# Down projection of a SwiGLU block as seven block products over all tokens

## The chip, the cores and the metric

One core of a Trainium2 chip. The metric is the device time of one execution in microseconds (us); of three runs of the kernel before, the median is 2898.46 us (2891.17 to 2900.06).

## The reference, cut to what matters

One decoder layer over 2048 prompt tokens and 8 sample tokens, all in float32. The mixer (HGRN2 and differential attention) comes first and is not touched. What follows is the feed-forward part:

```python
def swiglu(h, wg, wu, wd):
    return jnp.einsum('btf,fd->btd', jax.nn.silu(jnp.einsum('btd,df->btf', h, wg))
                      * jnp.einsum('btd,df->btf', h, wu), wd)
# hp = hp + swiglu(rmsnorm(hp, norm_ffn[l]), w_gate[l], w_up[l], w_down[l])
# y_prompt = rmsnorm(hp, norm_final)
# D_MODEL = 1024, D_FF = 2816; prompt 2048 tokens, sample 8 tokens
```

## The kernel before

A float32 product is made of three matmuls on rounded halves: each operand is split into a rounded part (a cast on ScalarE) and a rest (a subtraction on VectorE), and high x high, high x low and low x high are added in PSUM. This split stands behind every matrix product of the kernel, so each weight or token tile costs a cast and a subtraction before TensorE can use it.

**Gate/up** (`gate_up`, line 1171). The 2056 token columns (8 of the sample, then 2048) are cut into three groups of 688, 684 and 684 (`FG`). Per group `b_operands` loads the normed tokens into one staging tile (`xraw`) and makes the seven right operands of Strassen's scheme (Winograd's form: seven products of half-size blocks in place of eight), as 28 tiles `B`. Then for each of eleven pairs of feature tiles (256 features) and for both weights `a_operands` loads a 1024 x 256 block of weights (`raw_gate`, `raw_up`, one buffer each), forms four sums on VectorE and cuts seven left operands (`A`, ten buffers); `strassen` runs seven products of 4 x 3 matmuls with 342 or 344 columns, and VectorE puts the four result blocks together. The weights' sums are thus formed anew in each of the three groups. The features, silu(gate) x up, go to DRAM (`hd`) in two halves per pair.

**Down** (`down`, line 1201). Plain tiles: four groups of 512 tokens, two halves of 512 output columns each, and in each half 22 feature tiles x 4 token tiles x 3 matmuls of 512 columns. A weight tile (128 x 512) is loaded into `wraw` (three buffers), split into `w` (eight buffers) and used for the four token tiles; the 22 feature tiles of a token group are loaded into `hraw` and split into `ha` or `hb`. The eight sample tokens join the second token group as a fifth tile. `result` adds the product to the residual (`ya`), and after the second half norms, scales and stores the rows.

**What sets the order.** Instructions are written in program order; a planner then orders them per engine, giving an instruction its place as soon as its inputs and its buffer are free in its own time table, earlier ones first. Each engine, and SP's queue of DMA issues, then works strictly in that order: an instruction that waits holds up what is behind it. Loads are issued by SP, stores of gate/up by POOL (GpSimd). The buffers of a stage lie in the memory of the stage before; a tile there waits for the release of the tiles that it overlaps: `rb` (right side) holds `xraw`, `xtmp` and the operands `B`, and `rd` takes its place in down; `fa` (left) holds `A`, the raw weights and the feature tiles, and `fd` takes its place.

Of the kernel before, what the change touches and what calls it, by code (L numbers as in the profile page):

```python
# [9 lines left out]
F32 = mybir.dt.float32  # L10
# [9 lines left out]
P = 128  # L20
D = 1024
# [21 lines left out]
def layer_kernel(ctx, tc, x_prompt, x_sample, cache_k, cache_v, state_hgrn, page_table, w_in, w_out,  # L43
# [112 lines left out]
    hd = [[T(dp, [P, 2, b - a], F32, f"hd{a}_{c}") for c in range(NF // 2)] for a, b in FG]  # L156
# [66 lines left out]
    with ExitStack() as mx:  # L223
# [849 lines left out]
        def pieces(a, b):  # L1073

            out = []
            if a < NS:
                out.append((xtd_s, 0, NS, 0))
            for t in range(NT):
                lo, hi = max(a, NS + t * P), min(b, NS + (t + 1) * P)
                if lo < hi:  # L1080
                    out.append((xtd[t], lo - NS - t * P, hi - NS - t * P, lo - a))
            return out

# [8 lines left out]
        def b_operands(g):  # L1092
# [4 lines left out]
            for src, c0, c1, to in pieces(a, b):  # L1097
                sp.dma_start(raw[:, :, to:to + c1 - c0], src[:, :, c0:c1])
# [23 lines left out]
        def a_operands(fa, w, c, raw):  # L1122

            sp.dma_start(raw, w[:, c * 2 * P:(c + 1) * 2 * P].rearrange("(k p) f -> p k f", p=P))
            A11, A21, A12, A22 = (raw[:, k:k + 4, m * P:m * P + P] for k in (0, 4) for m in range(2))
# [7 lines left out]
            def sums(x, y, op):  # L1133
                s_ = T(fa, [P, 4, P], F32, "S", 4)
                dve.tensor_tensor(s_, x, y, op=op)
                return s_

            ops = {1: cut(A11)}
            S1 = sums(A21, A22, ALU.add)
            S2 = sums(S1, A11, ALU.subtract)  # L1140
            ops[6] = cut(S2)
            ops[7] = cut(sums(A11, A21, ALU.subtract))
            ops[5] = cut(S1)
            ops[4] = cut(A22)
            ops[3] = cut(sums(A12, S2, ALU.subtract))
            ops[2] = cut(A12)
            return ops
# [23 lines left out]
        def gate_up(fa):  # L1171
            fill = last_tokens()
            for g, (lo, hi) in enumerate(FG):
# [5 lines left out]
                for c in range(NF // 2):  # L1179
                    sg = [[T(fa, [P, TH], F32, "sg", 5)[:, 0:n] for j in range(2)] for i in range(2)]  # L1180
                    hh = [T(fa, [P, 2 * TH], F32, "hh", 3)[:, 0:2 * n].rearrange("p (j t) -> p j t", j=2) for i in range(2)]
# [5 lines left out]
                    def put_up(i, j, p, u, op):  # L1187
                        dve.tensor_tensor(hh[i][:, j], u, p, op=op)
                        dve.tensor_tensor(hh[i][:, j], hh[i][:, j], sg[i][j], op=ALU.mult)

                    us = [[T(fa, [P, TH], F32, tag, 2)[:, 0:n] for tag in ("s1", "s5", "u2", "u3")] for i in range(2)]
                    raws = [T(fa, [P, KT, 2 * P], F32, tag, 1) for tag in ("raw_up", "raw_gate")]
                    for w, put in ((w_gate, put_gate), (w_up, put_up)):
                        u_ = us.pop()
                        strassen(a_operands(fa, w, c, raws.pop()), B, n, put, u_)
                        pools["first"] = u_[1]
                        next(fill, None)
                    for i in range(2):
                        pool.dma_start(hd[g][c][:, i], hh[i].rearrange("p j t -> p (j t)"))

        def down(fd, rd):

            LATE = 15
            late = [T(rd, [P, 2, 512], F32R, "hb", LATE) for _ in range(LATE)]

# [5 lines left out]
            def weight(f, hs):  # L1211
                raw = T(rd, [P, 512], F32, "wraw", 3)
                sp.dma_start(raw, w_down[f * P:(f + 1) * P, hs])
                return halves(T(rd, [P, 2, 512], F32R, "w", 8), raw)

            def feature(f, c0):
                raw = T(rd, [P, 512], F32, "hraw", 3)
# [127 lines left out]
```

## Time and profile before

| what | value |
|---|---|
| profiled execution | 2899.44 us, span 2897.7 us |
| median of three runs | 2898.46 us |
| TensorE busy | 2790.8 us, 96% of the span |
| VectorE, ScalarE, GpSimd busy | 67%, 48%, 11% |
| bytes moved by DMA | 480.81 MB, 166 GB/s |
| mean granted TensorE clock | 0.982 of full speed |

Busy times overlap between engines. A matmul's listed duration includes its passage through the array, and the next starts before it ends; so the spacing of starts, not the duration, is the cost of one in a stream. A group's line ends with the idle time of the engine just before it and with what ended that idle time.

### The profile page before, as it was taken

What the parts mean: (1) busy time and instruction counts of PE and PEld (TensorE: products, weight loads), DVE (VectorE), ACT (ScalarE), POOL (GpSimd) and SP (SyncE); (2) the same over time, 40 slices, a digit from 0 to 9 for tenths busy, and PEclk for the clock granted to TensorE, in tenths of its full rate; (3) what the DMA queues carried; (4) which work ended last, traced back from release to release, by engine and by line L of the source; (5) the groups of instructions that cost most, each with busy time, mean ns of one, the idle gap of its engine ahead of it and who ended that gap; (6) DMA issues with size and microseconds to landing.
All of it is one profiled execution on the core that took longest, in us unless ns stands there. A gap on an engine that the chain in (4) does not pass through costs nothing.

```text
span 2897.7 us, 44200 instructions
## 1 busy us (share of the span) xinstructions
PE 2790.8 (96%) x16149; PEld 2524.7 (87%) x16149; DVE 1942.6 (67%) x4152; ACT 1393.3 (48%) x3256; POOL 322.3 (11%) x444
## 2 busy tenths in 40 slices
PE   8999999999999999998989999999999999999998
PEld 7887899888888788887779999999999997878886
DVE  6473577676766676862489889988988865525342
ACT  6422277665665656742564445444544434424232
POOL 2373400000000000011210000000000000000000
PEclk9999999999999999999999999999999999999999
DMA  6885896744644533334965333323233337726342
GB/s 226 310 280 174 248 296 197 235 150 148 209 135 143 184 134 134 103 124 151 326 207 170 117 102 123 126 102 110 100 102 107 103 119 239 221 90 228 129 160 77
DMA packets 311487, 480.81 MB, mean 166 GB/s; under 512 B 30659, under 2 KB 226293, under 8 KB 301542
## 3 DMA queue, kind: packets, MB, share of 16 engines
q1 hardware_dynamic: 281862, 364.13, 39.5%
q0 software_dynamic: 29408, 113.85, 10.8%
q8 instruction: 128, 2.10, 0.3%
q14 instruction: 89, 0.73, 0.1%
HBM read 359.81 MB, written 118.09 MB: 165 GB/s over the span
## 4 chain that ended last, share of the span: by engine, by line
PE 70%; issue 15%; DMA 8%; ACT 3%; DVE 2%; POOL 1%; SPq 1%; POOLq 0%; ACTq 0%; DVEq 0%
PE b L1155 10%; PE b L1156 10%; PE b L1157 10%; PE mm L315 7%; PE mm L316 7%; PE mm L317 7%; PE av L453 3%; PE sc L406 2%; PE th L536 2%; PE sc L408 2%; PE tpa L449 2%; PE b L1287 1%; PE b L1289 1%; PE b L1288 1%; DMA xn<-xnd 1%
## 5 line engine op out<-in xcount | busy, mean ns | idle before, releaser
L1155 PE MATMUL b<-B,A 128*128 128x342 f32 (+1 forms) x1848 | 593.5, 322 | 9.4 <-ACT B L1088 7.0
L1157 PE MATMUL b<-B,A 128*128 128x342 f32 (+1 forms) x1848 | 591.2, 320 | 0.7 <-DVE A L1130 0.7
L1156 PE MATMUL b<-B,A 128*128 128x342 f32 (+1 forms) x1848 | 591.0, 320 | 0.0
L315 PE MATMUL mm<-xn,w 128*128 128x512 f32 (+1 forms) x1120 | 405.1, 362 | 6.3 <-ACT hraw L486 3.1
L317 PE MATMUL mm<-xn,w 128*128 128x512 f32 (+1 forms) x1120 | 396.6, 354 | 0.0
L316 PE MATMUL mm<-xn,w 128*128 128x512 f32 (+1 forms) x1120 | 396.2, 354 | 0.0
L1155 PEld LDWEIGHTS b<-B,A 128*128 128x128 f32 x1848 | 350.3, 190 | 12.0 <-ACT B L1088 8.6
L1156 PEld LDWEIGHTS b<-B,A 128*128 128x128 f32 x1848 | 350.9, 190 | 0.0
L1157 PEld LDWEIGHTS b<-B,A 128*128 128x128 f32 x1848 | 349.3, 189 | 1.0 <-DVE A L1130 1.0
L1208 DVE TENSOR_TENSOR w<-wraw,w 128x512 fp32r<-128x512 f32 x176 | 121.2, 690 | 219.4 <-ACT w L1207 219.0
L412 DVE TENSOR_REDUCE nms<-sc 128x1 f32<-128x512 f32 (+3 forms) x320 | 188.3, 605 | 117.4 <-PE sc L408 59.3
L1129 ACT CAST A<-S 128x512 fp32r<-128x512 f32 x264 | 163.2, 621 | 213.0 <-PE b L1157 198.4
L315 PEld LDWEIGHTS mm<-xn,w 128*128 128x128 f32 x1120 | 215.4, 192 | 34.3 <-ACT hraw L486 4.4
L317 PEld LDWEIGHTS mm<-xn,w 128*128 128x128 f32 x1120 | 214.7, 192 | 27.1
L316 PEld LDWEIGHTS mm<-xn,w 128*128 128x128 f32 x1120 | 215.3, 192 | 24.9
L413 ACT ACTIVATE e<-sc,nms 128x512 f32<-128x512 f32 (+3 forms) x320 | 201.6, 635 | 67.4 <-DVE nms L412 65.2
L1207 ACT CAST w<-wraw 128x512 fp32r<-128x512 f32 x176 | 109.2, 621 | 250.5 <-PE b L1289 199.0
L1130 DVE TENSOR_TENSOR A<-S,A 128x512 fp32r<-128x512 f32 x264 | 181.3, 689 | 30.1 <-ACT A L1129 26.5
L1287 PE MATMUL b<-w,hb 128*128 128x512 f32 x480 | 186.2, 390 | 1.8 <-ACT hb L1207 1.8
L1288 PE MATMUL b<-w,hb 128*128 128x512 f32 x480 | 185.8, 389 | 0.0
L1289 PE MATMUL b<-w,hb 128*128 128x512 f32 x480 | 185.4, 390 | 0.0
L453 PE MATMUL av<-vb,pt 128*128 128x128 f32 x1088 | 155.6, 282 | 11.4 <-ACT pt L451 11.2
(379 smaller groups left out, 5558.8 us busy)
## 6 DMA issues: line engine op xcount, KB each, us to landing
w<-wd SPq DMA_DIRECT2D x48, 1024.0 KB, 5.0
wraw<-in_w_down_dram SPq DMA_DIRECT2D x176, 256.0 KB, 2.9
raw_gate<-in_w_gate_dram SPq DMA_DIRECT2D x33, 1024.0 KB
raw_up<-in_w_up_dram SPq DMA_DIRECT2D x33, 1024.0 KB, 5.3
wraw<-in_w_in_dram SPq DMA_DIRECT2D x40, 512.0 KB, 7.0
kb<-kd SPq DMA_DIRECT2D x40, 512.0 KB, 6.2
wd<-w SPq DMA_DIRECT2D x16, 1024.0 KB, 5.5
qst<-qd SPq DMA_DIRECT2D x128, 128.0 KB, 6.5
```

Source lines behind the costliest of these rows:

```text
L315: pe.matmul(bk[:, 0:n], wv[:, 0, kt], xk[:, 0, c0:c1], start=kt == 0, stop=False)
L316: pe.matmul(bk[:, 0:n], wv[:, 0, kt], xk[:, 1, c0:c1], start=False, stop=False)
L317: pe.matmul(bk[:, 0:n], wv[:, 1, kt], xk[:, 0, c0:c1], start=False, stop=kt == KT - 1)
L412: dve.tensor_reduce(nm, sc[:, 0:n], axis=AX.X, op=ALU.max, negate=True)
L413: act.activation(e[m][:, 0:n], sc[:, 0:n], AF.Exp, bias=nm, accum_out=c["z"][:, b, m:m + 1])
L453: pe.matmul(po[:, 0:P], pt[:, j * P:(j + 1) * P], it["v"][b][:, j], start=b == 0 and j == 0, stop=b == nb - 1 and j == n // P - 1)
L1155: pe.matmul(bk[:, 0:n], a[:, 0, k], b[:, 0, 0:n], start=k == 0, stop=False)
L1156: pe.matmul(bk[:, 0:n], a[:, 0, k], b[:, 1, 0:n], start=False, stop=False)
L1157: pe.matmul(bk[:, 0:n], a[:, 1, k], b[:, 0, 0:n], start=False, stop=k == 3)
L1287: pe.matmul(bk[t], h[f][:, 0, ts], w[f][:, 0], start=st, stop=False)
L1288: pe.matmul(bk[t], h[f][:, 0, ts], w[f][:, 1], start=False, stop=False)
L1289: pe.matmul(bk[t], h[f][:, 1, ts], w[f][:, 0], start=False, stop=en)
```

## The change

The features' own block sums are now made in gate/up, and down runs Strassen's scheme over blocks of 1024 tokens x 1408 features x 512 outputs.

- Gate/up: the weights' sums are formed in place in a seven-slot tile in the first group only (`sums7`), stored to DRAM (`wsd`), and loaded from there in the other two groups. `A` has eight buffers instead of ten, and the separate tiles for sums are gone. The features of a pair go into a seven-slot tile `hh`, where `sums7` adds three sums and a difference (four more VectorE operations per pair), and all seven slots are stored (`hd`). The token groups are mapped so that the two halves of a group hold tokens 1024 apart; the sample's features are copied out (`hsd`).
- Down: for each of seven products in the order 1, 6, 7, 5, 4, 3, 2, eight row blocks of 128 tokens x 11 feature pairs x 3 matmuls of 512 columns. The eleven weights of a product are each summed from one to four raw tiles (`SUM`). The features of a row block are one load of 128 x 11 x 128 values in runs of at most 512 bytes. Results stay in sixteen SBUF tiles `Y2` of 128 x 1024; each product is added where it belongs; the residual is added in product 5, rows 1024 to 2047 are finished in product 4 and rows 0 to 1023 in product 2. The sample runs beside the products 1, 5, 3 and 2 with the same weights.

```diff
-    hd = [[T(dp, [P, 2, b - a], F32, f"hd{a}_{c}") for c in range(NF // 2)] for a, b in FG]
+    hd = [T(dp, [P, 7, NF // 2, (b - a) // 2], F32, f"hd{a}") for a, b in FG]
+    hsd = T(dp, [P, NF, NS], F32, "hsd")
+    wsd = [[T(dp, [P, 7, 512], F32, f"wsd{m}_{c}") for c in range(NF // 2)] for m in range(2)]
...
+        def sums7(x):
+            tt = dve.tensor_tensor
+            tt(x[:, 3], x[:, 5], x[:, 1], op=ALU.add)
+            tt(x[:, 4], x[:, 3], x[:, 0], op=ALU.subtract)
+            tt(x[:, 5], x[:, 0], x[:, 5], op=ALU.subtract)
+            tt(x[:, 6], x[:, 2], x[:, 4], op=ALU.subtract)
+        SLOT = {1: 0, 6: 4, 7: 5, 5: 3, 4: 1, 3: 6, 2: 2}
...
-        def a_operands(fa, w, c, raw):
-            sp.dma_start(raw, w[:, c * 2 * P:(c + 1) * 2 * P].rearrange("(k p) f -> p k f", p=P))
+        def a_operands(fa, m, c, raw, g):
+            if g:
+                sp.dma_start(raw, wsd[m][c])
+            else:
+                w = (w_gate, w_up)[m]
+                for slot, k, col in ((0, 0, 0), (5, 0, 1), (1, 1, 1), (2, 1, 0)):
+                    at = (2 * c + col) * P
+                    sp.dma_start(raw[:, slot].rearrange("p (k f) -> p k f", k=4),
+                                 w[k * 512:(k + 1) * 512, at:at + P].rearrange("(k p) f -> p k f", p=P))
             def cut(x):
-                o = T(fa, [P, 2, 4, P], F32R, "A", 10)
+                o = T(fa, [P, 2, 4, P], F32R, "A", 8)
...
+            ops = {1: cut(raw[:, 0])}
+            if g == 0:
+                sums7(raw)
+                pool.dma_start(wsd[m][c], raw)
+            for p in (6, 7, 5, 4, 3, 2):
+                ops[p] = cut(raw[:, SLOT[p]])
...
+                    raws = [T(fa, [P, 7, 512], F32, tag, 1) for tag in ("raw_up", "raw_gate")]
...
+                            hh.append(T(fa, [P, 7, TH], F32, "hh", 2))
...
-                        pool.dma_start(hd[g][c][:, i], hh[i].rearrange("p j t -> p (j t)"))
+                    x = hh[0][:, :, 0:n]
...
+                    sums7(x)
+                    pool.dma_start(hd[g][:, :, c], x)
...
         def down(fd, rd):
+            NC = NF // 2
+            order = (1, 6, 7, 5, 4, 3, 2)
+            SUM = {1: ((0, 0, 1),), 6: ((1, 1, 1), (0, 1, -1), (0, 0, 1)), 7: ((1, 1, 1), (0, 1, -1)),
+                   5: ((0, 1, 1), (0, 0, -1)), 4: ((1, 1, 1), (0, 1, -1), (0, 0, 1), (1, 0, -1)), 3: ((1, 1, 1),), 2: ((1, 0, 1),)}
...
+            def weight(p, c):
+                got = None
+                for k, n, sign in SUM[p]:
+                    raw = T(rd, [P, 512], F32, "wraw", 4)
+                    sp.dma_start(raw, w_down[(2 * c + k) * P:(2 * c + k + 1) * P, n * 512:n * 512 + 512])
+                    if got is not None:
+                        dve.tensor_tensor(got, got, raw, op=ALU.add if sign > 0 else ALU.subtract)
+                    else:
+                        got = raw
+                return halves(T(rd, [P, 2, 512], F32R, "w", 16), got)
...
+            def feature(p, i):
+                raw = T(rd, [P, NC, P], F32, "hraw", 2)
+                for g, c0, c1, _, r in rows(0, i):
+                    sp.dma_start(raw[:, :, r:r + c1 - c0], hd[g][:, SLOT[p], :, c0:c1])
+                return halves(T(rd, [P, 2, NC, P], F32R, "h", 2), raw)
...
+            def residual(h, i):
+                res = T(fd, [P, D], F32, "res", 2)
...
+                y = Y2[h][i]
+                dve.tensor_tensor(y, y, res, op=ALU.add)
...
+            for p in order:
+                W = []
+                for i in range(8):
+                    A = feature(p, i)
+                    bk = bank()
+                    for c in range(NC):
+                        if i == 0:
+                            W.append(weight(p, c))
+                        pe.matmul(bk, A[:, 0, c], W[c][:, 0], start=c == 0, stop=False)
+                        pe.matmul(bk, A[:, 0, c], W[c][:, 1], start=False, stop=False)
+                        pe.matmul(bk, A[:, 1, c], W[c][:, 0], start=False, stop=c == NC - 1)
...
+                    if p == 1:
+                        act.copy(a[0], bk)
+                    elif p == 6:
+                        tt(a[1], a[0], bk, op=ALU.add)
+                    elif p == 7:
+                        tt(b[0], a[1], bk, op=ALU.add)
+                    elif p == 5:
+                        tt(b[1], b[0], bk, op=ALU.add)
+                        tt(a[1], a[1], bk, op=ALU.add)
+                        residual(1, i)
+                        residual(0, i)
...
+                    if p in (4, 2):
+                        h = 1 if p == 4 else 0
...
+                        finish(P, Y2[h][i])
+                        for g, c0, c1, t0, r in rows(h, i):
+                            sp.dma_start(yp[t0:t0 + c1 - c0], Y2[h][i][r:r + c1 - c0])
```

## Rows read from the trace of the kernel before

**Rows 1.** The page, busy time, share of the span and instructions per engine.
```profile
PE 2790.8 (96%) x16149; PEld 2524.7 (87%) x16149; DVE 1942.6 (67%) x4152; ACT 1393.3 (48%) x3256; POOL 322.3 (11%) x444
```

**Rows 2.** Stretches: length, busy per engine (instructions), granted clock, DMA share, GB/s.
```profile
1488.50:2376.60 888.10, 880.09 (x5560) 877.28 (x5560) 773.91 (x1388) 411.14 (x791) 38.92 (x70) 0.99 0.34 113
2376.60:2885.00 508.40, 502.39 (x2201) 409.04 (x2200) 216.62 (x318) 177.40 (x314) 17.07 (x18) 1.00 0.52 170
...
2110.00:2200.00 90.00, 90.00 (x576) 90.00 (x575) 79.36 (x143) 38.90 (x74) 4.32 (x8) 1.00 0.34 114
```

**Rows 3.** Groups by line and shape, TensorE in the down projection.
```profile
L1287 PE MATMUL b<-w,hb 128*128 128x512 f32 x480 | 186.2, 390 | 1.8 <-ACT hb L1207 1.8
...
L1287 PE MATMUL b<-w,ha 128*128 128x512 f32 x224 | 86.1, 391 | 4.2 <-ACT ha L1207 4.2
```

**Rows 4.** Timeline of TensorE around the stages' border: start, duration, engine, line, tiles.
```profile
2373.11 0.32 PE L1157 MATMUL b<-B,A 128*128 128x342 f32 x1
...
2376.40 0.32 PE L1157 MATMUL b<-B,A 128*128 128x342 f32 x1
2380.04 1.29 PE L1287 MATMUL b<-w,ha 128*128 128x512 f32 x4 [3.32 <-ACT ha L1207]
...
2384.48 1.08 PE L1287 MATMUL b<-w,ha 128*128 128x512 f32 x4
...
2388.58 0.39 PE L1287 MATMUL b<-w,ha 128*128 128x512 f32 x1
...
2391.53 0.39 PE L1288 MATMUL b<-w,ha 128*128 128x512 f32 x1
```

**Rows 5.** Timeline of VectorE at the start of gate/up, operations back to back.
```profile
1495.43 0.69 DVE L1130 TENSOR_TENSOR A<-raw_gate,A 128x512 fp32r<-128x512 f32 x1
1496.03 0.69 DVE L1130 TENSOR_TENSOR A<-S,A 128x512 fp32r<-128x512 f32 x1
...
1505.25 0.52 DVE L1184 TENSOR_TENSOR sg<-u,s 128x344 f32<-128x344 f32 x1
1505.68 0.52 DVE L1184 TENSOR_TENSOR sg<-u,b 128x344 f32<-128x344 f32 x1
```

**Rows 6.** Groups by line and shape, splits on VectorE and ScalarE.
```profile
L1208 DVE TENSOR_TENSOR w<-wraw,w 128x512 fp32r<-128x512 f32 x176 | 121.2, 690 | 219.4 <-ACT w L1207 219.0
L1207 ACT CAST w<-wraw 128x512 fp32r<-128x512 f32 x176 | 109.2, 621 | 250.5 <-PE b L1289 199.0 <-DMA wraw<-in_w_down_dram 49.5 <-DVE hb L1208 0.8
...
L174 DVE TENSOR_TENSOR w<-wraw,w 128x1024 fp32r<-128x1024 f32 x40 | 48.8, 1221 | 22.0 <-ACT w L173 21.7
L173 ACT CAST w<-wraw 128x1024 fp32r<-128x1024 f32 x44 | 46.0, 1046 | 18.9 <-DMA wraw<-in_w_in_dram 12.0 <-DMA wraw<-in_w_out_dram 5.7 <-issue 1.0
```

**Rows 7.** DMA issues: tiles, queue, count, KB each, median us from issue to landing.
```profile
wraw<-in_w_down_dram SPq DMA_DIRECT2D x176, 256.0 KB, 2.9
...
raw_up<-in_w_up_dram SPq DMA_DIRECT2D x33, 1024.0 KB, 5.3
...
xnd<-xn POOLq DMA_DIRECT2D x6, 2048.0 KB, 11.2
```

**Rows 8.** Stretches of 5 us at the start of the down projection.
```profile
2385.00:2390.00 5.00, 5.00 (x24) 4.12 (x23) 1.70 (x3) 1.66 (x4) 0.00 (x0) 1.00 1.01 382
...
2395.00:2400.00 5.00, 4.08 (x17) 2.77 (x16) 2.62 (x4) 2.34 (x4) 0.00 (x0) 1.00 0.79 204
2400.00:2405.00 5.00, 3.85 (x17) 2.84 (x17) 2.14 (x4) 2.02 (x3) 0.00 (x0) 1.00 0.64 164
...
2425.00:2430.00 5.00, 5.00 (x24) 4.14 (x23) 4.20 (x7) 3.70 (x6) 0.00 (x0) 1.00 0.91 285
```

**Rows 9.** Waits of SP's queue in the down projection: total us, times, longest.
```profile
SPq L1213 <- DVE w L1208: 232.1, 137, 3.8
...
SPq L1221 <- PE b L1157: 42.0, 1, 42.0
```

**Rows 10.** The gate/up product line: what ended TensorE's idle time (us, times).
```profile
  ACT B L1088: 15.6, 12
```

More of the change, by code (lines that the diff above doesn't have):

```diff
@@ new lines, in down, with rows @@
+            edge = [0, 340, 682, 1024]
+            def rows(h, i):
+                out = []
+                for g in range(3):
+                    lo, hi = max(edge[g], i * P), min(edge[g + 1], (i + 1) * P)
+                    if lo < hi:
+                        c0 = lo - edge[g] + (4 if g == 0 else 0)
+                        out.append((g, c0, c0 + hi - lo, columns(g, c0, c0 + hi - lo, h), lo - i * P))
+                return out
+            def feature(p, i):
[3 more added lines that the diff above has]
+                return halves(T(rd, [P, 2, NC, P], F32R, "h", 2), raw)
@@ new lines, in finish, with sample_products @@
+            def finish(n, y):
+                r = norm_rows(n, y[0:n], fd)
+                dve.scalar_tensor_tensor(y[0:n], y[0:n], r, gF[0:n], op0=ALU.mult, op1=ALU.mult)
+            Y2 = [[None] * 8 for _ in range(2)]
+            gF = hsm = ys_ = None
+            def sample_products(p, W):
+                k, n = {1: (0, (0, 1)), 2: (1, (0,)), 5: (0, (1,)), 3: (1, (1,))}[p]
+                bk = bank()
+                for c in range(NC):
+                    both = hsm[:, 2 * c + k].rearrange("p s t -> p (s t)")
+                    pe.matmul(bk[0:64], both, W[c][:, 0], start=c == 0, stop=False)
+                    pe.matmul(bk[0:64], both, W[c][:, 1], start=False, stop=c == NC - 1)
+                fold = T(fd, [P, 512], F32, "fold", 1)[0:32]
+                act.copy(fold, bk[32:64])
+                dve.tensor_tensor(fold, fold, bk[0:32], op=ALU.add)
+                for x in n:
+                    at = ys_[0:32, x * 512:x * 512 + 512]
+                    dve.tensor_tensor(at, at, fold, op=ALU.add)
@@ new lines, in down @@
+                        for g, c0, c1, t0, r in rows(h, i):
+                            sp.dma_start(yp[t0:t0 + c1 - c0], Y2[h][i][r:r + c1 - c0])
+                    if i == 2 and p in (1, 2, 3, 5):
+                        if p == 1:
+                            hsm = sample_features()
+                            ys_ = T(fd, [P, D], F32, "ys", 1)
+                            sp.dma_start(ys_[0:32], yd_s)
+                        sample_products(p, W)
+                        if p == 2:
+                            finish(32, ys_)
+                            sp.dma_start(ys, ys_[0:NS])
```

168 lines of the change are left out of this document (53 added, 115 removed).

## The prediction

> **What bounds the kernel now.** I read the page's busy shares first, then busy time by stage, then the instruction groups of the two stages that the change touches, then TensorE's own order of time, and last VectorE's, the DMA issues and SP's queue. TensorE is busy for 96% of the span [rows 1]. By stage [rows 2]: gate/up lasts from 1488.5 to 2376.6 us with TensorE busy 880 of 888 us, the down projection from there to 2885 with 502 of 508, and 12.7 us to the span's end follow almost without products. Both have a granted clock of 0.99 to 1.00, which is the 2.4 GHz level. Busy time counts pipelined matmuls double (each is listed with 390 ns), so I price a matmul by its spacing: from 2388.58 to 2391.53 us lie 13 steps of 0.2269 us for 512 columns, and from 2373.11 to 2376.40 lie 21 steps of 0.1567 us for 342 columns [rows 3, 4]. Down has (480 + 224) x 3 = 2112 prompt matmuls and the stretch has 2200 weight loads in all [rows 2], so 88 for the sample (22 x 2 x 2): 2200 x 0.2268 = 499.0 us. From the last gate/up product to the span's end is 521.1 us, so 22.1 us are not products: 12.7 us of tail and 9.4 us of gaps, mainly the first 3.5 us, slow matmuls behind them [rows 4] and crumbs. TensorE sets the end in both stages; fewer matmuls are paid back one for one as long as their operands come.
>
> **Down: what goes.** Seven products x 8 row blocks x 11 feature pairs x 3 = 1848 matmuls of the same shape (before: 2112). The sample's are 4 products x 11 x 2 = 88, as before. So 264 go: 264 x 0.2268 = 59.9 us off TensorE, all of it on the path. Bounds: 0 if operands bind instead, 59.9 if not.
>
> **Down: what comes.** One product keeps TensorE for 8 x 33 x 0.2268 = 59.9 us, one row block for 7.5 us.
> - Features: 56 loads of 128 x 1408 values (704 KB), two raw and two split buffers. Neighbours: 256 KB of weights land in 2.9 us, 1 MB in 5.3 us [rows 7], so 3 to 7 us against 7.5 us of products, with two blocks of lead. The cast of 1408 columns is about 1.4 us on ScalarE and the subtraction 1.6 us on VectorE (line through 512 columns, 621 and 690 ns, and 1024, 1046 and 1221 ns [rows 6]). Hidden; uncovered it would be 3 us per block.
> - Weights: 1, 3, 2, 2, 4, 1, 1 raw tiles per sum in the order 1, 6, 7, 5, 4, 3, 2, that is 14 x 11 = 154 loads of 256 KB instead of 176. The first row block of a product needs eleven weights in 7.5 us where the old loop needed one per 12 matmuls (2.7 us). Sixteen buffers leave five made ahead; the other six get a buffer as the last row block of the product before lets them go. From its first feature pair to the point where the eleventh weight is needed is about 13.5 us. ScalarE's wait of 199 us for old products [rows 6] and SP's 232 us for VectorE's release of raw buffers [rows 9] say that loads already run as far ahead as buffers allow, so I take that the new ones do too. The four raw buffers let three more sums be finished ahead, since a sum is made in place. Then for three weights there is a chain: buffer freed, load (2.9 + 0.3 us of issue), adds, cast, subtraction. For four raw tiles per sum it is about 5.3 us each: ready at 1.4 + 3.2 + 3.4 + 2 x 5.3 = 18.6 us, 5 us late. For three tiles it comes out at 14.8 us, 1 to 2 us late. For one and two, in time.
> - VectorE in product 5: per row block two additions from PSUM, two residual additions of 1024 columns, the feature's subtraction and, for product 4, its share of 8 sums of three additions and 5 subtractions. Back to back a 512-column operation goes every 0.60 us [rows 5], so 1.2 + 2.3 + 1.5 + 2.2 = 7.2 of 7.5 us. That is near the bound: what it delays is product 4's prefetch. I charge product 5 and the change to 4 together 15 us (5 to 30), the change to 6 four (0 to 8), other crumbs two.
> - Start: the first feature load of before waited 42 us at the head of SP's queue for gate/up's last product [rows 9], because of the memory it lay in. Now the first raw features lie where the token operands of gate/up were staged, which is free early; weights lie in operand memory that is freed product by product in the last 10 us. I take 5 us; 0 if all is early, 12 if the first feature load again starts at the last product (load and cast) and eleven weights then come at the 285 to 380 GB/s of a full DMA [rows 8].
> - Tail: again one block's add, norm, scale and store. Nothing.
>
> What the row shows of the clock: after the 3.3 us gap the first 12 matmuls took 2380.04 to 2384.48 us, 4.4 us instead of 2.7 [rows 4]: 1.7 us lost at the 1.2 GHz level. The crumbs that followed left it at 1.00 [rows 8]. The Trainium skill ("TensorE: Matmul & The Clock Gate", Part 1) says that throttled is the default state and that activity releases it. By it the stalls at products 6 and 4, if they fall in one piece each, cost about 3.4 us more; falling in crumbs, nothing. I expect crumbs, and the allowance of 15 us holds the difference.
>
> **Gate/up.** Matmuls unchanged. VectorE loses 4 sums x 22 per group of tokens in groups 2 and 3 (176 x 0.60) and gains 4 sums of 344 columns per feature pair (132 x 0.43 us [rows 5]). Per feature pair TensorE needs 168 x 0.157 = 26.4 us. VectorE before: 22 operations at 0.60 and 18 at 0.43, 20.9 us. After: 22.6 us in the first group, 17.8 us in the others. Still covered; no gain, since TensorE had no wait for it in 2110 to 2200 us [rows 2]. If VectorE's cover were gone, the four sums would cost 1.7 x 11 = 19 us in the first group. Operand buffers go from ten to eight: a cut is then still made six products (11 us) ahead.
> Transfers: in the first group a feature pair moves 2 x 1 MB of weights in, 2 x 1.75 MB of sums out and 1.2 MB of features out, 7.0 MB in 26.4 us or 265 GB/s. Later groups move 4.9 MB, 186 GB/s; before it was 113 [rows 2]. The DMA has carried 382 GB/s when full and 285 with short waits [rows 8], and a 2 MB store took 11.2 us [rows 7], so a single raw buffer (store 10, load 6, sums 3 us in a cycle of 26.4) is in time. I take +3 us for a rougher start, bounds -4 (the 16 us that TensorE waits for token operands [rows 10] shrink with VectorE's lighter load) and +25.
>
> **Sum.** -59.9 - 9.4 (old gaps) + 5 + 4 + 15 + 2 + 3 = -40.3 us. The profiled execution took 2899.4 us (span 2897.7), 1 us above the median of the runs; so 2859 us.
>
> **Rivals.**
> - *All operands come in time* (2833 us): -59.9 - 9.4 + 3. For it: five weights ahead and early memory at the start. Against it: product 4's four loads per weight, VectorE at 7.2 of 7.5 us.
> - *The first group of gate/up becomes bound by transfers* (2883 us): writes and short rows hold the DMA to about 245 GB/s, so 7.0 MB take 28.6 us instead of 26.4, 24 us over eleven pairs. For it: 164 to 204 GB/s at a DMA share of 0.64 to 0.79 [rows 8], which points to 257 at full share. Against it: 382 and 285 with less to wait for.
> - *SP's queue holds the weights back* (2922 us, slower): a load that waits for a buffer stands ahead of the rest and no weight is made ahead. A first row block then takes 256 KB at 285 GB/s = 0.92 us per raw tile: 10.1 us per tile of a sum, minus 7.5 us of products: 2.6 x 3 + 12.7 x 2 + 22.8 + 33 = 89 us, and -59.9 - 9.4 + 89 + 3 = +23. It decides when over three quarters of these loads are exposed. For it: the 42 us at the queue's head [rows 9]. Against it: the long waits of ScalarE for the old products show prefetch up to the buffers.
>
> **Chances.** Forecast 0.54 (own range 2840 to 2878), all in time 0.18, transfers 0.15, queue 0.10, and 0.03 for mixtures near the old time. From 2830 to 2888 us lie nearly all of the first, most of the second and third: 0.8. About 0.3% (9 us) is what a measurement can tell from no change: faster 0.87, same 0.04, slower 0.09.
>
> **What would show it.** Matmuls of the down line 1848 at the same 0.227 us; its stage near 478 us; gaps above a microsecond only where product 6 and product 4 begin, released by the weights' subtraction; the first down product within 5 us of gate/up's last; gate/up within 5 us of 888; DMA share near 0.75 in its first third. Wrong would be: TensorE gaps in every row block (features), gate/up's first third longer than 295 us (transfers or VectorE), or stalls at all product changes (queue).

## The result, and the profile after

The changed kernel takes 2948.69 us (median of four runs, 2944.66 to 2951.56) against 2899.26 us before on the same chip: a ratio of 1.0174, 95% interval 1.0149 to 1.0200. It is slower by about 50 us, where 40 us less was forecast. The execution profiled below took 2945.9 us, span 2944.1.

A correction to the description ahead: the two halves of a token group are not 1024 tokens apart. Half 0 of the three groups holds tokens 0 to 339, 680 to 1021 and 1364 to 1705, half 1 the 340 or 342 that follow each. ("Rows 0 to 1023" and "1024 to 2047" are thus the rows of half 0 and of half 1.) So the 128 rows of a product's block do not line up with the 128-token tiles of `yd`, in which the residual lies, and for twelve of the sixteen blocks the residual is loaded in two to four pieces, of 2 to 86 rows. That turns out to matter.

The page of after (as [rows 1]): TensorE is busy 32 us less, although 59.9 us of matmuls went, and for a smaller share of a longer span.

```profile
PE 2758.3 (94%) x15885; PEld 2483.7 (84%) x15885; DVE 1929.8 (66%) x4099; ACT 1362.3 (46%) x3181; POOL 328.0 (11%) x443
```

The stretches of after (as [rows 2]: length, busy per engine, granted clock, DMA share, GB/s): all of gate/up, down from its first to its last product, gate/up's first and last token group; then the same two groups in the kernel before.

```profile
1489.10:2378.30 889.20, 878.12 (x5558) 874.33 (x5558) 705.37 (x1340) 410.89 (x836) 51.17 (x69) 0.99 0.69 218
2378.60:2936.10 557.50, 476.81 (x1936) 374.95 (x1936) 271.98 (x312) 146.83 (x194) 11.80 (x17) 0.91 0.65 176
1488.30:1794.20 305.90, 297.31 (x1864) 294.22 (x1865) 255.94 (x487) 136.16 (x302) 29.71 (x47) 0.99 0.81 278
2088.50:2378.00 289.50, 289.50 (x1848) 289.50 (x1848) 216.85 (x412) 130.44 (x249) 10.46 (x11) 1.00 0.68 178
```

```profile
1488.50:1783.20 294.70, 293.67 (x1864) 292.67 (x1865) 260.95 (x467) 142.97 (x275) 14.64 (x25) 0.99 0.38 126
2079.70:2376.60 296.90, 293.30 (x1850) 292.37 (x1848) 249.80 (x450) 129.15 (x247) 12.42 (x23) 0.99 0.30 100
```

Gate/up as a whole is where it was (889.2 us), but the first token group takes 11 us more and the last 7 us less. Down takes 557.5 us instead of 508.4, though its matmuls are the 1848 that were forecast (as [rows 3]; the idle time at the end is new):

```profile
L1325 PE MATMUL b<-w,h 128*128 128x512 f32 x616 | 250.0, 410 | 43.5 <-ACT h L1243 25.3
L1327 PE MATMUL b<-w,h 128*128 128x512 f32 x616 | 249.7, 407 | 25.9 <-DVE h L1244 25.9
...
L1326 PE MATMUL b<-w,h 128*128 128x512 f32 x616 | 250.0, 406 | 11.5 <-DVE w L1244 11.5
```

The same columns for the seven products of down, in order 1, 6, 7, 5, 4, 3, 2 (a product ends with its last result update):

```profile
2378.30:2474.00 95.70, 73.61 (x288) 56.63 (x288) 41.80 (x53) 27.46 (x39) 0.95 (x1) 0.88 0.79 202
2474.00:2540.90 66.90, 63.25 (x266) 50.35 (x265) 33.41 (x41) 17.71 (x21) 0.00 (x0) 0.95 0.67 187
2540.90:2609.00 68.10, 63.02 (x266) 50.69 (x265) 32.20 (x39) 17.20 (x20) 0.00 (x0) 0.95 0.63 171
2609.00:2716.60 107.60, 79.11 (x306) 60.65 (x304) 58.43 (x69) 18.06 (x19) 0.00 (x0) 0.87 0.71 188
2716.60:2806.20 89.60, 68.04 (x245) 52.02 (x246) 48.95 (x56) 25.94 (x42) 4.98 (x7) 0.77 0.66 190
2806.20:2871.20 65.00, 65.00 (x287) 52.49 (x286) 27.79 (x31) 19.09 (x24) 0.95 (x1) 1.00 0.56 151
2871.20:2936.10 64.90, 64.87 (x286) 52.12 (x284) 29.60 (x27) 21.62 (x34) 4.92 (x8) 1.00 0.41 121
```

A full-speed product lasts 264 x 0.2268 = 59.9 us, with the sample's 22 matmuls (products 1, 5, 3, 2) 64.9. What is above that I call its gap: 30.8, 7.0, 8.2, 42.7, 29.7, 0.1 and 0.0 us, together 118.5. The last two columns say that on average over a product the DMA engines are not full (share 0.79 at most); shorter stretches may be.

So against the time before: -59.9 (matmuls) - 9.4 (old gaps) + 118.5 + 1.1 (gate/up) - 4.7 (tail, 8.0 us instead of 12.7) = +45.6, which gives 2945.0 of the 2945.9 measured. The forecast had 26 us (5 + 4 + 15 + 2) in the place of the 118.5.

What TensorE waits for in down (us in total, times, longest): 80.9 us of waits, on all four kinds of operand half. The other 37.6 us are matmuls at a lower granted clock, 0.77 to 0.95 in the five products with gaps: 153 matmuls that start at least 0.38 us after the one before, waits taken off, hold 36.0 of them.

```profile
PE b L1327 <- DVE h L1244: 25.9, 7, 8.1
PE b L1325 <- ACT h L1243: 25.3, 8, 7.0
PE b L1325 <- ACT w L1243: 18.2, 7, 7.1
PE b L1326 <- DVE w L1244: 11.5, 2, 7.5
```

And what ScalarE and VectorE wait for there: casts of weights wait for sums, and VectorE waits for raw tiles and for residual rows.

```profile
ACT w L1243 <- DVE wraw L1253: 166.1, 31, 18.1
...
DVE wraw L1253 <- DMA wraw<-in_w_down_dram: 63.0, 40, 6.0
DVE y L1294 <- DMA res<-yd: 49.2, 11, 8.9
```

A stretch of product 5 shows how such a wait gets to TensorE (start, duration, engine or queue, line; in brackets the idle time before it):

```profile
2667.71 0.62 ACT L1243 CAST w<-wraw 128x512 fp32r<-128x512 f32 x1 [18.10 <-DVE wraw L1253]
2668.23 1.36 ACT L1243 CAST h<-hraw 128x1408 fp32r<-128x1408 f32 x1
...
2673.72 8.44 SPq L1251 DMA_DIRECT2D wraw<-in_w_down_dram  x1
2682.29 1.23 DVE L1294 TENSOR_TENSOR y<-y,res 128x1024 f32<-128x1024 f32 x1 [8.59 <-DMA res<-yd]
...
2687.69 1.62 DVE L1244 TENSOR_TENSOR h<-hraw,h 128x1408 fp32r<-128x1408 f32 x1
...
2689.36 0.79 PE L1327 MATMUL b<-w,h 128*128 128x512 f32 x1 [5.86 <-DVE h L1244]
```

VectorE stands 8.6 us at a residual addition; the sums for product 4 and the feature's subtraction stand behind it, and TensorE waits for the latter. ScalarE stands 18.1 us at a weight of product 4, and the cast of product 5's own features, which needs no weight, comes right after it. Prefetch for the next product is thus in front of the current product's work. From 2655 to 2701 us the chain of waits in product 5 (start, us, what) is almost all residual:

```profile
2655.26 13.05 DMA res<-yd
2668.40 1.24 DVE y L1294
2669.99 14.67 DMA res<-yd
2684.75 1.24 DVE y L1294
2687.08 14.11 DMA res<-yd
```

Two buffers: a load is issued when an addition frees one, and takes 13 to 15 us to land. Why so long shows in the DMA view of 2669 to 2685 us, in 40 slices of 0.4 us (busy tenths, then GB/s):

```profile
DMA  9699769998988689999998221111111111397155
GB/s 160 252 328 225 236 215 282 230 246 210 195 230 256 124 230 278 230 188 215 204 221 146 60 69 51 51 51 51 51 51 51 46 56 51 128 307 261 41 120 143
```

For 4 us a tenth of the sixteen engines is busy, at 51 GB/s: two engines, with everything else through (from 2678.8 to 2681.2 us two packets are in flight, each one residual row of 4096 bytes). From the fourth block on, product 5 has five residual loads with a piece of 86 rows; 86 rows (344 KB) at 51 GB/s are 6.9 us. The three loads in the chain are of 84 and 42 rows: each was issued 3 to 5 us behind an 86-row piece and its addition came within 3 us of that piece's. In the same time SP needs 8.44 us for one weight issue (above), so the next loads wait too.

### The profile page after: what moved, and what is told of

It reads as the page before. It is cut to its first block, busy times and chain, and to the rows that moved or that the text cites. A ratio compares the mean times of both kernels' runs of the same rounds, so it can differ in the third digit from the quotient of the medians.

```text
span 2944.1 us, 43533 instructions
## 1 busy us (share of the span) xinstructions
PE 2758.3 (94%) x15885; PEld 2483.7 (84%) x15885; DVE 1929.8 (66%) x4099; ACT 1362.3 (46%) x3181; POOL 328.0 (11%) x443
## 4 chain that ended last, share of the span: by engine, by line
PE 60%; DMA 16%; issue 9%; DVE 8%; ACT 4%; SPq 2%; POOL 1%; DVEq 0%; POOLq 0%; ACTq 0%
PE b L1177 7%; PE b L1179 7%; PE b L1178 7%; PE mm L317 6%; PE mm L318 6%; PE mm L319 6%; PE av L455 3%; DMA wraw<-in_w_down_dram 3%; DMA raw_up<-in_w_up_dram 2%; DMA res<-yd 2%; PE th L538 2%; PE sc L408 2%; PE sc L410 2%; PE tpa L451 1%; PE b L1327 1%
## 5 line engine op out<-in xcount | busy, mean ns | idle before, releaser
L1325 PE MATMUL b<-w,h 128*128 128x512 f32 x616 | 250.0, 410 | 43.5 <-ACT h L1243 25.3
L1327 PE MATMUL b<-w,h 128*128 128x512 f32 x616 | 249.7, 407 | 25.9 <-DVE h L1244 25.9
L414 DVE TENSOR_REDUCE nms<-sc 128x1 f32<-128x512 f32 (+3 forms) x320 | 188.7, 606 | 118.6 <-PE sc L410 61.2
L1326 PE MATMUL b<-w,h 128*128 128x512 f32 x616 | 250.0, 406 | 11.5 <-DVE w L1244 11.5
L1159 ACT CAST A<-raw_gate 128x512 fp32r<-128x512 f32 x231 | 140.4, 620 | 125.0 <-PE b L1179 91.1
L1159 ACT CAST A<-raw_up 128x512 fp32r<-128x512 f32 x231 | 141.5, 621 | 110.8 <-PE b L1179 90.6
L1325 PEld LDWEIGHTS b<-w,h 128*128 128x128 f32 x616 | 121.2, 198 | 77.7 <-ACT h L1243 31.2
L1160 DVE TENSOR_TENSOR A<-raw_gate,A 128x512 fp32r<-128x512 f32 x231 | 157.4, 687 | 40.2 <-ACT A L1159 39.9
L1327 PEld LDWEIGHTS b<-w,h 128*128 128x128 f32 x616 | 121.4, 197 | 55.7 <-DVE h L1244 30.2
```

Of the source, the lines that this page charges most:

```text
L414: dve.tensor_reduce(nm, sc[:, 0:n], axis=AX.X, op=ALU.max, negate=True)
L1325: pe.matmul(bk, A[:, 0, c], W[c][:, 0], start=c == 0, stop=False)
L1326: pe.matmul(bk, A[:, 0, c], W[c][:, 1], start=False, stop=False)
L1327: pe.matmul(bk, A[:, 1, c], W[c][:, 0], start=False, stop=c == NC - 1)
```

## The experiments

All are edits of the changed kernel; "before" ran beside each. Gaps in us by product; the last two columns are the sum over all seven products and the time: the median of four runs for after and where a ratio is given below, else one run. Four runs of one kernel spread by 4.5 to 14.6 us, so smaller differences between single runs are read from the gaps and waits.

| kernel | 1 | 6 | 7 | 5 | 4 | sum | time |
|---|---|---|---|---|---|---|---|
| after | 30.8 | 7.0 | 8.2 | 42.7 | 29.7 | 118.5 | 2948.7 |
| one raw tile per sum | 29.9 | -0.1 | 0.0 | 23.0 | 9.1 | 62.1 | 2890.5 |
| features by row block | 25.0 | 9.2 | 2.9 | 35.8 | 28.7 | 101.9 | 2940.5 |
| features by GpSimd's queue | 28.3 | 9.4 | 3.4 | 43.3 | 35.8 | 115.7 | 2946.4 |
| residual by GpSimd's queue | 31.8 | 8.4 | 7.8 | 19.0 | 24.2 | 91.3 | 2925.5 |
| residual in one load | 31.4 | 10.9 | 7.1 | 22.7 | 22.6 | 95.2 | 2922.9 |
| eight raw buffers | 22.1 | 0.0 | -0.1 | 30.9 | 17.0 | 68.5 | 2897.4 |
| sums made in gate/up | 29.8 | -0.1 | 0.0 | 23.5 | 6.0 | 59.3 | 2887.7 |
| eight buffers + one load | 22.8 | -0.1 | -0.1 | 15.9 | 1.2 | 38.3 | 2868.2 |
| the same + additions spread | 23.1 | -0.1 | 0.0 | 10.8 | -3.3 | 29.1 | 2857.4 |
| all four | 24.9 | 0.2 | 0.0 | 0.9 | 0.2 | 24.8 | 2852.5 |

(Product 3 has -1.5 to 0.5 and product 2 at most 0.1; with the features by GpSimd's queue -4.0 and -0.5. A product ends with its last result update, so a late update can move some us from one product's gap to the next, below zero too.)

**Which part of the work is late.** Four kernels, one edit each. The expectations weigh three theories. A: feature loads of short runs hold SP's queue. B: VectorE stands at the residual additions, whose loads are late. C: the weights' sums have too few raw buffers. First, a sum takes only its first raw tile and leaves the others out:

```diff
-                for k, n, sign in SUM[p]:
+                for k, n, sign in SUM[p][:1]:
```

> Leaves out of each weight sum all raw tiles but the first: 77 loads of 256 KB and 77 additions on VectorE go, and products 6, 7, 5 and 4 use one raw tile instead of a sum. Theory C: gaps of 6, 7, 4 and 5 go, product 1's 31 us stay, total about 2860. Theory B (the residual alone): products 6, 7 and 4 lose theirs, product 5 keeps 30 us or more, total about 2890. Theory A: as C for 6 and 7, part of 5 stays since the residual's loads stand behind feature loads, about 15 us, total about 2875.

Measured 2890.5 us: 56 of the 118.5 us go with the sums' further loads and additions; the start (29.9), half of product 5 (23.0) and a third of product 4 (9.1) do not. The time is theory B's, but product 5 keeps less than its 30 us; theory C's 2860 is missed.

Features in DRAM by row block, so that a partition's are one run of 5632 bytes:

```diff
-    hd = [T(dp, [P, 7, NF // 2, (b - a) // 2], F32, f"hd{a}") for a, b in FG]
+    hd = [T(dp, [P, 7, NF // 2, P], F32, f"hd{i}") for i in range(8)]
...
-                for g, c0, c1, _, r in rows(0, i):
-                    sp.dma_start(raw[:, :, r:r + c1 - c0], hd[g][:, SLOT[p], :, c0:c1])
+                sp.dma_start(raw, hd[i][:, SLOT[p]])
```

> Same work; the features lie in DRAM by row block, so that a feature load is one run of 5632 bytes per partition instead of eleven of at most 512, and the short runs are in gate/up's stores. In the changed kernel the down stage has 119 us of gaps: about 31 in product 1, 7 in 6, 8 in 7, 43 in 5, 30 in 4, none in 3 and 2. Theory A (short runs: a feature load keeps SP's queue of DMA issues for 7 to 8 us, what stands behind it comes late): nearly all of them shrink, down stage below 490 us, total 2850 to 2875. Theory B (a ring in product 5: VectorE stands at the residual addition, whose load SP issues behind weight loads that wait for VectorE): 60 us or more stay in products 5 and 4, total above 2895. Theory C (weight sums through four raw buffers): the gaps of 6, 7 and 4 stay, total above 2895. Rival to all: the short runs now slow gate/up, whose stage grows by over 15 us.

Measured 2940.5 us, gate/up 10 us longer (899.1). SP's issues of 7 to 8 us are gone, but VectorE still waits 41.1 us for residual rows. Theory A's 2850 to 2875 is missed: the short runs are a small part.

The feature loads, and then the residual loads, given to GpSimd's queue:

```diff
-                    sp.dma_start(raw[:, :, r:r + c1 - c0], hd[g][:, SLOT[p], :, c0:c1])
+                    pool.dma_start(raw[:, :, r:r + c1 - c0], hd[g][:, SLOT[p], :, c0:c1])
```

> The changed kernel with the feature loads of down issued by GpSimd's queue instead of SP's; runs and bytes are the same. Theory A as a matter of the queue (SP is held): gaps of all products shrink by more than half, total 2860 to 2890. Theory A as a matter of the DMA engines' time on short runs: little changes, total 2925 to 2945. Theory B: products 5 and 4 keep 60 us, total above 2905. Theory C: 6, 7 and 4 keep theirs, total above 2900.

2946.4 us: the queue of the features is no cause.

```diff
-                        sp.dma_start(res[r:r + n], yd[t0 // P][t0 % P:t0 % P + n])
+                        pool.dma_start(res[r:r + n], yd[t0 // P][t0 % P:t0 % P + n])
```

> The changed kernel with the residual's loads issued by GpSimd's queue instead of SP's, nothing else. Theory B: the 73 us of gaps in products 5 and 4 fall below 20, total about 2885. Theory A: product 5 gains part, but weight loads still stand behind the feature loads, some 35 us stay, total about 2905. Theory C: product 4's 30 us stay, product 5 gains, total about 2910. In all three the gaps of products 1, 6 and 7 (46 us) stay.

2925.5 us: product 5's gap falls from 42.7 to 19.0, VectorE's wait for residual rows from 49.2 to 7.2 us. So about half of product 5's gap hangs on the residual's loads by SP. Theory B's 2885 is missed, as the other half and product 4's 24.2 stay. The pieces are the same, but on this queue up to 16 of their rows are in flight at once, and they land after 3.1 to 10.3 us (median 6.7), where the chain above has 13 to 15.

**What makes them late.** `yd` as one tensor, so that a block's residual is one load of 128 rows for twelve of sixteen blocks (20 loads instead of 31; the others are still cut where a token group ends):

```diff
-    yd = [T(dp, [P, D], F32, f"yd{t}") for t in range(NT)]
+    yd = T(dp, [SEQ, D], F32, "yd")
...
-                    while c0 < c1:
-                        n = min(c1 - c0, P - t0 % P)
-                        sp.dma_start(res[r:r + n], yd[t0 // P][t0 % P:t0 % P + n])
-                        c0, t0, r = c0 + n, t0 + n, r + n
+                    n = c1 - c0
+                    sp.dma_start(res[r:r + n], yd[t0:t0 + n])
```

> The changed kernel with the residual kept as one DRAM tensor, so that the load of a row block is one transfer of 128 rows (two where a token group ends inside the block) instead of pieces of 2 to 86 rows cut at the old tiles' borders. Theory B as a matter of those pieces (few rows land late): VectorE's 49 us of waits for the residual fall below 20 and the gaps of products 5 and 4 from 72 us to about 45, total about 2920. If it is the place of these loads in SP's queue and not their shape, the waits stay above 40 us and the total above 2935.

2922.9 us, near the expected 2920: the cut alone is 20 of product 5's 42.7 us, nearly what the other queue gave. VectorE still waits 22.4 us for residual rows, and 14.7 of them are at the two blocks that still have a piece of 86 rows. The load of one of them, issued at 2672.6 us, took 20.0 us to land.

Eight raw weight buffers instead of four:

```diff
-                    raw = T(rd, [P, 512], F32, "wraw", 4)
+                    raw = T(rd, [P, 512], F32, "wraw", 8)
```

> The changed kernel with eight raw weight buffers instead of four. Theory C as a matter of buffers: a sum of four tiles no longer waits for the sum before it; the gaps of products 6, 7 and 4 fall by more than half, product 1's by a third, total about 2905. If it is the number of loads and additions that stand in the in-order queues, and not the buffers, the gaps of 5 and 4 stay above 60 us together and the total above 2930.

2897.4 us, 51 us from one number: the gaps of products 6 and 7 vanish, ScalarE's wait for sums falls from 166.1 to 39.0 us. Product 4's gap falls from 29.7 to 17.0, less than the half that was expected.

The sums made in gate/up's second and third token group and kept in DRAM (`wdd`), one load per weight:

```diff
+                    if g:
+                        u = 11 * (g - 1) + c
+                        down_sums(fa, u // 2, u % 2 * 256)
...
+                got = T(rd, [P, 512], F32, "wraw", 4)
+                sp.dma_start(got, wdd[c][:, {1: 0, 6: 4, 7: 3, 5: 5, 4: 6, 3: 1, 2: 2}[p]])
```

> The down weights' sums are made in the second and third token group of gate/up (22 steps of four half-width loads, four operations on VectorE, one store to DRAM, through the feature tile's buffers), and each weight in down is one load. If the sums inside down cost what leaving them out gave back (56 us), down falls by 50 to 60 us and gate/up grows by 0 to 8, total 2890 to 2900. If gate/up becomes bound by its transfers (54 GB/s more on 186), its stage grows by over 15 us and the total stays above 2905. Product 5 keeps about 23 us and product 1 about 30.

2887.7 us; gate/up does not pay for it (887.6 us).

**Together.** Sums early, one load, eight buffers, and half of the residual additions moved from product 5 to product 3:

```diff
                         residual(1, i)
-                        residual(0, i)
...
                     elif p == 3:
                         tt(a[1], a[1], bk, op=ALU.add)
+                        residual(0, i)
```

> The early sums, the residual as one tensor with the first half's rows added in product 3 instead of 5, and eight raw weight buffers. If sums, residual and the start's raw buffers are the three causes, product 5's gap falls below 6 us, 6, 7 and 4 have none, product 1 has 10 to 20 us, total 2850 to 2865, below the kernel before. If product 1's start is bound by the bytes of weights, features, residual and norm vector together, it keeps 25 to 30 us and the total is about 2870.

2859.6 us in one run. Product 5 keeps 0.9 us, as expected, but product 1 has 24.8 instead of 10 to 20. Four more runs of the same kernel:

> The same kernel as the one look with sums made in gate/up, eight raw buffers, residual in one load and spread over products 5 and 3, now timed in rounds against the kernel before. Theory C and D alike: 2859 us +- 5, ratio to before 0.986 +- 0.003; the saving left out against the forecast's -59.9 - 9.4 is the gap of 25 us in product 1.

2852.5 us (2852.0 to 2860.9), ratio to before 0.9846 (0.9828 to 0.9863). Only product 1 has a gap left. Then the same without the sums in gate/up, and that one without the moved additions:

> The down projection's weight sums are again made where they are used, as in the changed kernel; it has eight raw weight buffers, the residual rows of a block in one load, and half of the residual additions moved from product 5 to product 3. Theory C (in-order queues: the delay is that prefetch of weights stands behind late residual loads, and with four raw buffers goes no further): buffers and residual take most of the 118 us of gaps, the three changes alone give 2871 us +- 8, with product 5's gap under 8 us and product 4's near the 17 us of the run with eight buffers. Theory D (the sums themselves, 154 loads and their adds, are too much for VectorE and the queue wherever they stand): product 4 and 5 keep 15 us of gaps or more each, 2890 us or more.

2857.4 us in one run, 14 us less than theory C's 2871; product 5 keeps 10.8 us and product 4 has no gap. Theory D's 2890 is missed: the sums are not too much for VectorE or the queue, once their raw tiles run eight ahead. Its products 1, 6, 5 and 4 show it; after product 1 (0.90) the clock is back at 0.98 to 1.00:

```profile
2379.40:2467.40 88.00, 70.54 (x288) 55.36 (x288) 48.14 (x64) 28.31 (x41) 0.95 (x1) 0.90 0.95 252
2467.40:2527.20 59.80, 59.80 (x265) 49.56 (x264) 31.62 (x38) 17.62 (x20) 0.00 (x0) 1.00 0.70 196
...
2587.10:2662.80 75.70, 71.92 (x309) 57.48 (x308) 57.58 (x75) 20.05 (x22) 0.00 (x0) 0.98 0.94 266
2662.80:2719.40 56.60, 56.60 (x251) 46.76 (x250) 35.48 (x38) 25.69 (x40) 4.51 (x7) 1.00 0.75 220
```

> Only eight raw weight buffers and the residual of a block in one load; all sixteen residual additions stay in product 5, all sums are made where they are used. Theory C (prefetch that stands behind late loads in the order of the queues): once loads run eight raw tiles ahead and the residual comes in time, VectorE's 7.2 of 7.5 us per block in product 5 is all that is left: 2862 us +- 6 (the 2857 with the additions spread, and 5 us more), ratio to before 0.987 +- 0.003, product 5 and 4 together 10 to 20 us late. Rival G (VectorE's load in product 5 binds, and spreading it was what helped): product 5 and 4 together stay at the 48 us that they have with eight buffers alone, 2890 us or more.

2868.2 us, ratio 0.9889 (0.9864 to 0.9913); products 5 and 4 are 17.1 us late, as expected. Rival G falls: the number of raw buffers and the form of one DRAM tensor make the changed kernel faster than before.

**The start.** Five kernels for product 1's gap of 22 to 31 us. Down's sums one feature pair earlier in gate/up (on the kernel with all four edits):

```diff
-                    if g:
-                        u = 11 * (g - 1) + c
+                    u = 11 * g + c - 10
+                    if 0 <= u < 22:
```

> The same with the down weight sums one feature pair earlier in gate/up (from the last pair of the first token group to the pair before the last of the third), so that the last store before the down projection is that of the features alone. Theory E (the first feature load of product 1 waits in SP's queue 20.5 us for the store of the last gate/up pair, whose buffer its memory overlaps): the load is issued about 5 to 12 us earlier, product 1's gap falls from 24.8 to 12 to 18 us, 2850 us +- 5. Rival F (product 1 is bound by the 3.7 MB it must move, and by the queue of SP): gap within 3 us of 24.8, 2859 us.

2859.9 us, ratio 0.9868 (0.9851 to 0.9884). The first feature load is issued 10.5 us before gate/up's last product instead of 12.4 us after it in the first run with all four edits, and the gap falls to 18.9, between both forecasts. But gate/up lasts 895.5 us: 7 us given back, no gain.

The features of two row blocks ahead of the first weights, on the kernel of 2857.4 us:

```diff
+                ahead = [feature(p, i) for i in range(2)] if p == 1 else []
                 for i in range(8):
-                    A = feature(p, i)
+                    A = ahead[i] if i < len(ahead) else feature(p, i)
```

> The kernel with eight raw buffers, whole residual rows and spread additions, with one more edit: in product 1 the features of the first two row blocks are asked for ahead of the first weights, so that SP issues the second block's load with the first one instead of behind eight weight loads (where it was issued at 2382.8 us, 3.4 us after gate/up's last product, and took 18.5 us to land). Theory H (order of SP's queue at the start): the second block is split before gate/up ends, the 11.3 us wait goes, product 1's gap falls from 23 to 8 to 14 us, and the time from 2857 to 2847 us +- 6. Rival I (bytes and short runs bind the start: eleven weights and three blocks, some 5 MB, must land in the first 20 us, in whatever order): the gap moves to the third block or the last three weights and stays within 4 us of 23, 2857 us.

2863.1 us (ratio 0.9871, 0.9854 to 0.9887), gap 27.5: theory H falls, and rival I is near (it gave 23 with 4 us either way). The stall moved to the last three weights, issued at 2406.7 us. They stood in SP's queue behind product 5's residual load, which waited 14.4 us for a feature store. So next the residual and the norm vector by GpSimd's queue, with the features first and without:

```diff
-                    sp.dma_start(res[r:r + n], yd[t0:t0 + n])
+                    pool.dma_start(res[r:r + n], yd[t0:t0 + n])
...
-                            sp.dma_start(gF, norm_final[None].broadcast_to([P, D]))
+                            pool.dma_start(gF, norm_final[None].broadcast_to([P, D]))
```

> The kernel that asks for two blocks of features first (2863 us), with one more edit: the residual rows and the final norm's vector go by GpSimd's queue instead of SP's. Theory J (SP's queue, head of line: the residual load of product 5 stood at its head until 2399.7, waiting for gate/up's last feature store to release memory, and the weights 9 to 11 of product 1 were issued at 2406.7 behind it): the three weights are issued at about 2391, product 1's gap falls from 27.5 to 10 to 16 us, 2850 us +- 6. Rival I (bytes): gap 23 or more, 2858 us or more.

> The same queue change on the kernel with eight raw buffers, whole residual rows and spread additions (2857 us), without the features first. Theory J: the wait of 11.3 us for the second block's features remains (18.5 us from issue to landing), the three last weights come earlier; gap 16 to 21 us instead of 23, 2853 us +- 6. Rival I: gap within 3 us of 23.

2853.7 us (ratio 0.9849, 0.9832 to 0.9865), gap 21.7; and 2857.5 us, gap 25.5. The weights were issued at 2402.1 us, not at 2391: three feature issues took 15 us. So theory J explains 6 us of the gap with the features first, and none without (25.5 against 23.1). What both kernels gain is in product 5, whose gap falls to 2.5 and 2.4 us, from 11.8 and 10.8. The ten microseconds 2390 to 2400 in after, and in the kernel with features first and residual by GpSimd:

```profile
2390.00:2400.00 10.00, 4.43 (x12) 3.12 (x13) 1.90 (x2) 3.42 (x5) 0.00 (x0) 0.66 1.14 172
```

```profile
2390.00:2400.00 10.00, 10.00 (x37) 8.03 (x36) 3.31 (x6) 2.00 (x4) 0.00 (x0) 0.78 1.22 185
```

The DMA engines are full (share 1.14, 1.22) and carry 172 and 185 GB/s. In this stretch that speaks for the transfer itself, not its order. The last kernel changes the runs alone, on the kernel of 2857.4 us (the edit of the features by row block):

> The kernel with eight raw buffers, whole residual rows and spread additions, with the features kept in DRAM by row block, so that a partition's features are one run of 5632 bytes instead of eleven of at most 512. Theory H: the second block's load is still issued behind eight weights, at about 2383, and lands some 10 us sooner at most; product 1's gap 15 to 23 us, gate/up 10 us longer as in the run with this layout alone, 2855 to 2868 us. Rival I (the short runs bind the start): product 1's gap falls to 12 us or less.

2864.9 us: product 1's gap is 15.7 instead of 23.1, and a later stretch carries 292 GB/s at a share of 0.81, but gate/up, whose stores are now cut, takes 899.6 us.

```profile
2400.00:2410.00 10.00, 8.83 (x32) 6.58 (x31) 3.75 (x5) 2.78 (x4) 0.00 (x0) 0.86 0.81 292
```

In this one run short runs are thus a third of the start's gap (5.8 of 30.8 us with the layout alone). The rest, 16 to 19 us in the best case, stays open between the bytes (eleven weights and three blocks, about 5 MB), SP's issues, and a third candidate that no run removed, the weights' memory. In the changed kernel SP's queue stands at the second weight load for gate/up's last product, and the features of the second block, behind it, are issued only then:

```profile
SPq L1251 <- PE b L1179: 12.3, 1, 12.3
2379.73 13.96 DMA hraw<-hd
```

## Why the prediction was wrong, point by point

- **The matmuls that go** (-59.9): right, 1848 at 0.227 us.
- **Gate/up** (+3): +1.1, but by luck in part. The first token group takes 305.9 us instead of 294.7, so the sign of being wrong (a first third above 295 us) did come; the other two groups give 2 and 7 us back. The rival of a transfer-bound first group has 11 of its 24 us. TensorE waits there 7.8 us for weight halves and 2.6 for a feature tile, and VectorE 48.5 us for raw weights, whose next load waits for the store of the sums in the same buffer. No run separates bandwidth from that single buffer.
- **Weights** ("I take that the new ones do too"; 4 us for the change to product 6, part of the 15 for 5 and 4): the step that failed first. The old kernel's long waits for buffers were read as proof that loads run ahead, but its weights had one raw tile each. With four buffers and up to four tiles per sum they did not, and eight buffers gave back 50 us of gap. The price of one link was right (5.3 us for four raw tiles; from 2737.8 to 2753.2 us product 4's weights come 5.1 us apart), the number of links was not: at least five weights are late there, where the sum had three. I priced a late weight only where its product begins. In the engines' fixed order it stands in front of the current product's features, so it stops the product before.

```profile
2737.81 1.22 PE L1325 MATMUL b<-w,h 128*128 128x512 f32 x2 [2.28 <-ACT w L1243]
...
2743.01 1.22 PE L1325 MATMUL b<-w,h 128*128 128x512 f32 x2 [2.27 <-ACT w L1243]
```

- **VectorE in product 5** (7.2 of 7.5 us): the busy time was right (58.4 us in product 5's eight blocks), what it lacked was a wait. The residual loads were not in the sum at all; cut into pieces they cost some 20 us there and hold VectorE 49.2 us. With whole rows and weights ahead, products 5 and 4 are 17.1 us late, against the 15 forecast.
- **Start** (5, at most 12): 30.8. The price was taken from full-rate transfers of 285 to 382 GB/s [rows 8]; with runs of at most 512 bytes the same engines carried 172 to 239 in the first 20 us. The first features were early, as forecast (asked for at 2338.9 us), and the first matmul came 0.24 us after gate/up's last. But the weights' memory did not come free product by product: the second weight load waited 12.3 us for the last one, the second matmul 3.95 us for its weight, and the features behind it took 14 us to land.
- **The clock** (3.4 us at most, hidden in the allowance): 37.6 us. I had thought of single stalls or of crumbs that cost nothing. What came were 24 waits of 0.2 to 8.1 us, often close together: in product 4, 2735 to 2756 us, five or six matmuls follow each wait of 2.1 to 2.3 us, the granted clock is 0.50, which is the 1.2 GHz level, and matmuls start 0.43 us apart.

```profile
2735.00:2756.00 21.00, 12.15 (x26) 7.12 (x24) 12.38 (x19) 4.31 (x8) 0.00 (x0) 0.50 0.62 205
```

- **Tail** (0): 4.7 us shorter, not foreseen.
- **The queue rival** (2922, slower) had the sign and part of the mechanism. SP's queue did stand at weight loads that waited for earlier raw tiles and their readers, 122.9 us in the lines below and 61.2 with eight buffers. But by the rival all product changes stall; products 3 and 2 have no gap and 6 and 7 only 7 to 8 us. And it has no place for the residual, half of product 5's gap.

```profile
SPq L1251 <- DMA wraw<-in_w_down_dram: 52.2, 25, 5.5
SPq L1251 <- DVE wraw L1253: 36.3, 53, 2.3
SPq L1251 <- DVE w L1244: 34.4, 40, 4.3
```

With eight buffers, whole residual rows and spread additions the design takes 2857.4 us, against the 2859 that were forecast. That the two agree is luck in part: of this kernel's 29.1 us of gaps the start has 23.1, where the forecast had 5, and all the rest 6, where it had 21.

## What to carry to other kernels

When a change turns one load per operand into several with arithmetic between, count the raw buffers in tiles per operand, and price a late prefetch at whatever stands behind it on each in-order engine, not only at its own consumer. List every load that the new order needs, also those that were there before, with the number of rows in each piece. If gaps appear, add the slowed matmuls behind them to their price.

## What the runs showed of the hardware

- A load of 86 rows by SP's queue ran on two DMA engines at 51 GB/s, while the other fourteen had nothing to do. The Trainium skill ("DMA: Bandwidth & Descriptors", Why a DMA increments its semaphore by 16 and not by 1) says that the largest number up to 16 that divides the slowest dimension is the number of engines: 2 for 86, 14 for 42. The trace agrees for SP's queue, with its share of a tenth; by that rule rows are best cut in multiples of 16. By GpSimd's queue the same pieces had up to 16 rows in flight and landed in 6.7 us (median).
- A DMA share above 1 does not mean much data: 172 GB/s while features were loaded in runs of at most 512 bytes (share 1.14), 382 GB/s in the kernel before at 1.01 [rows 8].
- An issue on SP, 0.36 us in the median, took 6.5 to 9.3 us behind feature loads of short runs, at the start and in product 5. With features in one run per partition, or by GpSimd's queue, no issue of down took over 2 us; yet 101.9 and 115.7 us of gaps stayed, so these issues alone cost little.
